# Feed-forward up: the weights' high part against both stream parts in one 512-column matmul

## The chip, the cores and the metric

The kernel runs on one core of one Trainium2 chip. The metric is the device time of one execution in microseconds (us). The engines are named as in the profile: PE (TensorE, matmuls), PEld (its weight loads), DVE (VectorE), ACT (ScalarE), POOL (GpSimd) and SP (SyncE, which here issues most DMAs).

## The reference

A stream x of 256 tokens by 1024 features passes two blocks of two layers each. Every layer of the first block has a mixer and one feed-forward; every layer of the second has a feed-forward, a mixer (state space, then windowed attention), an attention to a memory of 256 tokens and another feed-forward. That makes six feed-forwards. Everything is float32. The lines that matter here:

```python
# first block, per layer: a convolution of width 3 over the tokens on all 2 * 2816 columns
up = depthwise_conv(h @ ffn_w_up[l], ffn_conv_w[l], ffn_conv_b[l])
f = (jax.nn.silu(up[..., :D_FF]) * up[..., D_FF:]) @ ffn_w_down[l]
h = layer_norm(DEEPNORM_ALPHA * h + f, ln_ffn_g[l], ln_ffn_b[l])

# second block, twice per layer
def swiglu(h, wi, wo):
    gate, up = jnp.split(h @ wi, 2, axis=-1)
    return (jax.nn.silu(gate) * up) @ wo
```

D_FF is 2816, so the up projection has 1024 x 5632 weights and the down projection 2816 x 1024.

## The kernel before

All activations stay on the chip, and the weights are streamed once. To keep float32 accuracy, each operand of a matmul is split into a high and a low part (`load` for weights, `split` for activations): ACT rounds the raw values to the high part (L111, a cast), DVE subtracts it from the raw ones for the low part (L112). A product is then three matmuls (`mm3`, L126 to L128): high by high, high by low, low by high.

Weights come in pieces of 1 MB, 128 partitions by 2048 columns. SP issues one DMA for a piece into one of three raw buffers, and ACT and DVE split it in steps of 512 columns (`CUT`) into one of four high and one of four low buffers. A buffer is free again when PE's last matmul on the piece is done.

The stream stands transposed as xh and xl, two tiles of 128 partitions x 8 x 256 (feature tile k, tokens). Each norm writes them through PE transposes into a "tr" bank, which ACT and DVE read out.

The accumulator memory has eight banks of 512 float32 columns: four under the name "acc", two "up", two "tr".

A feed-forward (`ffn`) has 22 blocks b of 128 gate and 128 up columns. Blocks 0 and 1 are made token by token in `first`, since the first token tile is normed earlier than the second. For b from 2 to 21, `up(b)` loads one piece (8 tiles of k by 256 columns), takes one "up" bank of 2 x 256 columns and computes the gate half and the up half of the block in it by `mma`: eight steps of k for each half, and in each step three matmuls with a 128x128 tile of weights as the stationary operand and 256 tokens as the moving one. `evac` reads the bank: with the convolution by one ACT and two DVE operations for each half (L283 to L285); then SiLU on ACT, the product on DVE (L290), and the split into gh and gl, tiles of two blocks that `G[j]` holds.

`down(j, t)` multiplies `G[j]` as the stationary operand with 256 rows of the down projection, 512 columns at a time, for token tile t. The loop over j from 1 to 10 issues two ups and, from j = 2, the down of j - 2; the last two downs follow token tile by token tile, and `fin(t)` adds the residual and norms the tile while PE goes on with the other one. A round below is two ups and one down.

The program is written in the order above. A planner turns it into one queue per engine: it takes the instructions by that order as their operands and buffers come free, by its own costs of each, and sets the semaphores. Each engine then works its queue in order.

Of the kernel before, what the change touches and what calls it, by code (L numbers as in the profile page):

```python
# [26 lines left out]
# order in which the parts of the first block's mixer are issued  # L27
MIX1 = "D0 A0 D1 A1 Q0 v16 Q1 U d1 S0 v18 b1 S1 d0 c b0 o3 a v28 o2"
MIX1_OUT = (1, 0)
# and those of the state-space mixer  # L30
SSD = "t z0 C z1 p0 z2 x0 B x2 x1 p1 e0 x3 w0 w1 y0 z3 o4 o5 e1 p2 p3 o0 o1 w3 y1 w2 o7 o6"
SSD_OUT = (2, 3)
# of the windowed attention and of the attention to the memory
# [3 lines left out]
# column offsets of the packed per-layer input projection of the first block  # L37
WIN_A, WIN_D, WIN_Q, WIN_SV, WIN_U = 0, 4096, 6912, 11008, 13056
# packed rows, read as broadcasts: first block, per layer
BR1 = dict(g6=(0, 384), gcq=(384, 576), gckv=(576, 704), svg=(704, 960), svb=(960, 1216))  # L40
BR1_N = 1216
# second block
BR_SSD = dict(dtb=(0, 16), alog=(16, 32), dsk=(32, 48))
BR_SWA = dict(gq=(0, 64), gk=(64, 128), sink=(128, 144))
# constants that depend on shapes alone
# [3 lines left out]
# per-partition parameters  # L49
# [12 lines left out]
class Kern:  # L62
# [38 lines left out]
    def load(self, src, n):  # L101
        """One piece of a weight stream: raw float32, then the two exact 12-bit parts."""
        nc = self.nc
        k = src.shape[0]
        r = self.wraw.tile([P, 2048], F32, name="wr", tag="wr")[:k, :n]
        nc.sync.dma_start(out=r, in_=src)
        h = self.whi.tile([P, 2048], F32R, name="wh", tag="wh")[:k, :n]
        l = self.wlo.tile([P, 2048], F32R, name="wl", tag="wl")[:k, :n]
        for c in range(0, n, CUT):
            s = slice(c, min(n, c + CUT))  # L110
            nc.scalar.copy(h[:, s], r[:, s])  # L111
            nc.vector.tensor_tensor(out=l[:, s], in0=r[:, s], in1=h[:, s].bitcast(F32), op=ALU.subtract)  # L112
        return h, l

    def loadk(self, src, k, n):
        h, l = self.load(src, k * n)
        return h.rearrange("p (k n) -> p k n", k=k), l.rearrange("p (k n) -> p k n", k=k)
# [5 lines left out]
    def mm3(self, out, sh, sl, mh, ml, first, last):  # L123
        """out += (sh+sl).T @ (mh+ml), the parts being exact."""
        mm = self.nc.tensor.matmul
        mm(out, sh, mh, start=first, stop=False)  # L126
        mm(out, sh, ml, start=False, stop=False)  # L127
        mm(out, sl, mh, start=False, stop=last)  # L128

    def mmb(self, out, t, wp, c0, c1):  # L130
        """Token-major projection of tile t of the stream: out [128 tok, c1-c0]."""
        xh, xl = self.xT
        kk = 0
        for h, l in wp:
            for k in range(h.shape[1]):
                s = slice(t * P, (t + 1) * P)
                self.mm3(out, xh[:, kk, s], xl[:, kk, s], h[:, k, c0:c1], l[:, k, c0:c1], kk == 0, kk == 7)
                kk += 1

    def mma(self, out, wp, c0):  # L140
        """Feature-major projection of 128 columns: out [128 feat, 256 tok]."""
        xh, xl = self.xT
        kk = 0
        for h, l in wp:
            for k in range(h.shape[1]):
                self.mm3(out, h[:, k, c0:c0 + P], l[:, k, c0:c0 + P], xh[:, kk, :], xl[:, kk, :], kk == 0, kk == 7)
                kk += 1

    def rstd(self, ss, n, scale, eps):
        """(ss*scale + eps) ** -0.5 over [128, n], in place."""  # L150
        nc = self.nc
        v = self.wk.tile([P, 8], F32, name="rv", tag="rv", bufs=4)[:, :n]
        r = self.wk.tile([P, 8], F32, name="rr", tag="rr", bufs=4)[:, :n]
        nc.vector.tensor_scalar(out=v, in0=ss, scalar1=scale, scalar2=eps, op0=ALU.mult, op1=ALU.add)  # L154
        nc.gpsimd.tensor_tensor(out=r, in0=v, in1=self.mh[:, 0:1].to_broadcast([P, n]), op=ALU.pow)  # L155
        return r
# [6 lines left out]
    def ln_stats(self, src, width):  # L163
        """mean and rstd of [128, width]"""
        nc = self.nc
        nb = (width + 511) // 512
        st = self.wk.tile([P, 2, 6], F32, name="bst", tag="bst", bufs=3)
        mv = self.wk.tile([P, 2], F32, name="mv", tag="mv", bufs=3)
        for i in range(nb):
            nc.vector.bn_stats(out=st[:, i, :], in_=src[:, i * 512:min(width, (i + 1) * 512)])  # L170
        nc.vector.bn_aggr(out=mv, in_=st[:, :nb, :])
        r = self.rstd(mv[:, 1:2], 1, 1.0, LN_EPS)
        return mv[:, 0:1], r[:, 0:1]

    def new_xT(self):
        self.xT = (self.wk.tile([P, 8, T], F32R, name="xh", tag="xh", bufs=1),
                   self.wk.tile([P, 8, T], F32R, name="xl", tag="xl", bufs=1))

    def transposes(self, src, n, dst_h, dst_l, w=P, rows=P):
        """src [128, n*w] -> dst [w, n, 128] split"""  # L180
        pt = self.bank("tr", [P, 4, P])
        for k in range(n):
            self.nc.tensor.transpose(pt[:w, k, :], src[:, k * w:(k + 1) * w], self.ident)  # L183
        self.split(pt[:w, :n, :], dst_h, dst_l)
# [5 lines left out]
    def norm_ln(self, t, g, b, xT=True):  # L190
        """x[t] <- layer norm of x[t]; then its transposed split"""
        nc, x = self.nc, self.x[t]
        m, r = self.ln_stats(x, D)
        for n in range(2):
            s = slice(n * 512, (n + 1) * 512)
            nc.vector.scalar_tensor_tensor(out=x[:, s], in0=x[:, s], scalar=m, in1=g[:, s], op0=ALU.subtract, op1=ALU.mult)
            nc.vector.scalar_tensor_tensor(out=x[:, s], in0=x[:, s], scalar=r, in1=b[:, s], op0=ALU.mult, op1=ALU.add)
            if xT:
                self.to_xT(x[:, s], n, t)
# [15 lines left out]
    def projector(self, wsrc, nk):  # L215
        """x += oT.T @ w in nk pieces of 256 rows; returns piece(j, oh, ol, kb, tiles) and the banks"""
# [18 lines left out]
    def project(self, oh, ol, wsrc, order, early, fin):  # L235
        """the whole of it; token tile 0 finishes first"""
# [19 lines left out]
    def finisher(self, mode, post, last=False):  # L256
        """post(t): the norm that opens the next stage"""
        def fin(t, acc):
            self.residual(t, acc, mode)
            if t == 0 and not last:  # L260
                self.new_xT()
            post(t)
        return fin

# [1 line left out]
    def ffn(self, wi, wo, conv, fin, nj=11):  # L266
        nc, tc = self.nc, self.tc
        with tc.tile_pool(name="ffn", bufs=2) as fp:
            G = {}

# [39 lines left out]
            def up(b):  # L310
                w = self.loadk(wi[:, b * 2048:(b + 1) * 2048], 8, 256)
                pu = self.bank("up", [P, 2, T])
                for h in range(2):
                    self.mma(pu[:, h], [w], h * P)
                evac(b, pu)
# [5 lines left out]
            def downw(j):  # L321
                WD[j] = self.loadk(wo[:, j * 2048:(j + 1) * 2048], 2, 1024)
# [25 lines left out]
    def softmax(self, sp, sc, nh, w, scale, ri):  # L348
        """sc [128 q, nh, w] in PSUM -> exp(scale*(sc - max)) in SBUF; ri <- 1/sum"""
# [10 lines left out]
    def rope(self, sp, src, nh, q, C, S, out):  # L360
        """out = rotate(src [128, nh, 4q]) with C, S [128, 4q]"""
# [14 lines left out]
    def mixer1(self, l, fin):  # L376
# [3 lines left out]
        with tc.tile_pool(name="mx", bufs=1) as sp:  # L380
# [11 lines left out]
            # A: gated, width-31 convolution over tokens  # L392
# [47 lines left out]
            # D: latent projections  # L440
# [52 lines left out]
            # B: grouped-query attention; heads lie in the order 0 2 1 3  # L493
# [25 lines left out]
            def attend(scores, vget, scale, kb, qt):  # L519
                """scores(u, m, qs): operands of member m of head pair u"""  # L520
# [31 lines left out]
            # C: spatial gating  # L552
# [88 lines left out]
    def xattn(self, i_, fin):  # L641
        nc, tc, a = self.nc, self.tc, self.a
        with tc.tile_pool(name="xa", bufs=1) as sp:
# [9 lines left out]
            def query(i):  # L653
                """query columns of half i // 2, token tile i % 2"""
# [45 lines left out]
            def out(i):  # L700
                """piece i // 2 of the output projection, token tile i % 2"""
# [12 lines left out]
    def ssd(self, fin):  # L714
# [6 lines left out]
        with tc.tile_pool(name="sd", bufs=1) as sp:  # L721
# [19 lines left out]
            def gate_z(i):  # L741
                """silu(z), column half i // 2, token tile i % 2"""
# [15 lines left out]
            def steps(_):  # L758
                """dt = softplus(raw + bias); cumulative sums of dt * a within each chunk"""
# [9 lines left out]
                # log(1 + e) = 2 atanh(e / (2 + e)), |argument| <= 1/3  # L769
# [70 lines left out]
            def decays(g):  # L840
                """exp(acs[l] - acs[s]) * (C B^T), transposed; and the decays to the chunk's end"""
# [23 lines left out]
            def core(g):  # L865
# [6 lines left out]
                # state carried out of the first chunk  # L872
# [29 lines left out]
            # pooling branch  # L902
# [61 lines left out]
    def swa(self, fin):  # L964
        nc, tc, a = self.nc, self.tc, self.a
        tr = nc.tensor.transpose
        with tc.tile_pool(name="sw", bufs=1) as sp:
# [16 lines left out]
            def qkv(i):  # L984
                """column group i // 2 (k and v, then the query halves), token tile i % 2"""
# [32 lines left out]
            def attend(i):  # L1018
                """query tile i // 4, half b of the heads, pair of slot pairs ip"""
# [43 lines left out]
            def out(i):  # L1063
                """piece i // 2 of the output projection, token tile i % 2"""
# [55 lines left out]
def _kmajor(w, c0, c1):  # L1120
    """columns c0:c1 of w [K, N] as [128, K/128, c1-c0]"""
# [8 lines left out]
def _group(w, c0, c1):  # L1130
    """a column group of w [1024, N] as two pieces of four row tiles"""
# [61 lines left out]
def pack(inp):  # L1193
# [4 lines left out]
    pcol = lambda v: v.reshape(-1, P).T  # [.., n*128] -> [128, ..n]  # L1198
# [36 lines left out]
    # heads of the windowed attention, in the order that pairs an even key head with an odd one  # L1235
# [24 lines left out]
```

## Time and profile before

| | us |
|---|---|
| median of 3 runs | 1865.55 |
| the runs | 1864.16, 1865.55, 1871.57 |
| span of the profiled execution | 1871.3 |
| PE busy in it | 1807.8 |
| DVE busy | 1244.9 |
| ACT busy | 1000.6 |

The span runs from the first to the last instruction of the profiled execution. Its own time as a run is not listed apart; the slowest run lies 0.27 us above the span. Busy time is the union of an engine's instructions, and the end of a matmul is modelled, so matmuls that follow each other closely overlap in the rows: their starts tell the pace, not their durations. The mean granted clock of TensorE over the span was 0.989 of full speed.

### The profile page before, as it was taken

The page shows a single profiled execution, that of the slowest core. Times are in us where ns is not written, and L with a number is a line of the kernel's source. Part 1 is how long each engine was busy: PE and PEld are TensorE (multiplying, and loading weights), DVE is VectorE, ACT ScalarE, POOL GpSimd, SP SyncE. Part 2 cuts the span into 40 slices and gives each one's busy share as a digit, 9 for nine tenths or more (in the row PEclk, how much of TensorE's full clock was granted, in tenths as well). Part 3 has the DMA queues.
Part 4 walks back from the last instruction along what each step waited for, and adds up shares of the span by engine and source line. Part 5 has one row for each costly group of instructions (what it writes and reads, how often), then busy time and mean ns, then how long its engine had stood idle before and what let it go on. Part 6 is the DMA issues. An engine that isn't in the chain of part 4 may idle for free.

```text
span 1871.3 us, 29875 instructions
## 1 busy us (share of the span) xinstructions
PE 1807.8 (97%) x11664; PEld 1615.5 (86%) x11664; DVE 1244.9 (67%) x2523; ACT 1000.6 (53%) x2178; POOL 67.1 (4%) x85
## 2 busy tenths in 40 slices
PE   6999999999999999999999999999999999999999
PEld 5777999977899989998988779999999977789998
DVE  6489877778977785555677766545645566775553
ACT  5565655556565554445674555444544457655442
POOL 0000000010000000000000000000000010000000
PEclk9999999999999999999999999999999999999999
DMA  8623755442765545554434536555555552435551
GB/s 312 209 94 110 248 181 180 150 163 68 236 203 180 191 161 191 181 187 162 141 119 147 182 136 214 183 187 194 169 183 194 186 189 102 158 135 188 197 182 68
DMA packets 50750, 320.93 MB, mean 172 GB/s; under 512 B 5616, under 2 KB 8560, under 8 KB 14896
## 3 DMA queue, kind: packets, MB, share of 16 engines
q1 hardware_dynamic: 46160, 311.63, 48.6%
q10 hardware_dynamic: 4448, 7.37, 1.2%
q8 instruction: 92, 1.51, 0.3%
q14 instruction: 50, 0.41, 0.1%
HBM read 315.84 MB, written 3.15 MB: 170 GB/s over the span
## 4 chain that ended last, share of the span: by engine, by line
PE 82%; DVE 9%; ACT 4%; POOL 2%; issue 2%; DMA 1%; SPq 0%; POOLq 0%; ACTq 0%
PE up L128 14%; PE up L126 14%; PE up L127 14%; PE acc L127 11%; PE acc L128 11%; PE acc L126 11%; DVE wl L112 3%; POOL rr L155 2%; PE tr L183 2%; ACT wh L111 1%; DVE ca L418 1%; DMA wr<-in_ffn_w_up_dram 1%; DVE xn L212 1%; PE up L1053 1%; PE up L539 1%
## 5 line engine op out<-in xcount | busy, mean ns | idle before, releaser
L112 DVE TENSOR_TENSOR wl<-wr,wh 128x512 fp32r<-128x512 f32 x1135 | 737.1, 682 | 416.6 <-ACT wh L111 412.2
L111 ACT CAST wh<-wr 128x512 fp32r<-128x512 f32 x1135 | 644.9, 618 | 499.3 <-issue 298.5
L128 PE MATMUL up<-xh,wl 128*128 128x256 f32 x2112 | 601.5, 285 | 3.9 <-DVE wl L112 3.9
L126 PE MATMUL up<-xh,wh 128*128 128x256 f32 x2112 | 602.4, 285 | 0.0
L127 PE MATMUL up<-xl,wh 128*128 128x256 f32 x2112 | 600.3, 284 | 0.0
L128 PEld LDWEIGHTS up<-xh,wl 128*128 128x128 f32 x2112 | 408.0, 193 | 5.1 <-DVE wl L112 4.9
L126 PEld LDWEIGHTS up<-xh,wh 128*128 128x128 f32 x2112 | 408.3, 193 | 2.5 <-issue 0.2
L127 PEld LDWEIGHTS up<-xl,wh 128*128 128x128 f32 x2112 | 408.0, 193 | 2.4
L128 PE MATMUL acc<-wh,gl 128*128 128x512 f32 x528 | 208.7, 395 | 0.0
L127 PE MATMUL acc<-wl,gh 128*128 128x512 f32 x528 | 208.4, 395 | 0.0
L126 PE MATMUL acc<-wh,gh 128*128 128x512 f32 x528 | 208.2, 394 | 0.0
L127 PE MATMUL acc<-wl,xh 128*128 128x512 f32 (+2 forms) x336 | 130.0, 388 | 0.4 <-DVE wl L112 0.4
L126 PE MATMUL acc<-wh,xh 128*128 128x512 f32 (+2 forms) x336 | 129.5, 389 | 0.4 <-ACT xh L120 0.3
L128 PE MATMUL acc<-wh,xl 128*128 128x512 f32 (+2 forms) x336 | 128.6, 384 | 0.0
L128 PEld LDWEIGHTS acc<-wh,gl 128*128 128x128 f32 x528 | 99.4, 188 | 23.0
L126 PEld LDWEIGHTS acc<-wh,gh 128*128 128x128 f32 x528 | 99.7, 189 | 20.7
L127 PEld LDWEIGHTS acc<-wl,gh 128*128 128x128 f32 x528 | 99.4, 188 | 20.7
L155 POOL TENSOR_TENSOR rr<-rv,mh 128x1 f32<-128x1 f32 (+4 forms) x66 | 59.2, 898 | 1483.1 <-DVE rv L154 1460.1
L120 ACT CAST gh<-g 128x256 fp32r<-128x256 f32 x132 | 53.4, 406 | 58.3 <-DVE g L290 58.3
L126 PEld LDWEIGHTS acc<-wh,xh 128*128 128x128 f32 x336 | 64.5, 192 | 11.6 <-ACT xh L120 1.3
L127 PEld LDWEIGHTS acc<-wl,xh 128*128 128x128 f32 x336 | 64.4, 192 | 10.7 <-DVE wl L112 0.9
L128 PEld LDWEIGHTS acc<-wh,xl 128*128 128x128 f32 x336 | 64.4, 192 | 10.2
(323 smaller groups left out, 2217.7 us busy)
## 6 DMA issues: line engine op xcount, KB each, us to landing
wr<-in_ffn_wi_dram SPq DMA_DIRECT2D x88, 1024.0 KB, 4.9
wr<-in_ffn_w_up_dram SPq DMA_DIRECT2D x44, 1024.0 KB, 5.0
wr<-in_ffn_wo_dram SPq DMA_DIRECT2D x44, 1024.0 KB, 4.8
wr<-in_ffn_w_down_dram SPq DMA_DIRECT2D x22, 1024.0 KB, 4.8
wr<-in_ssd_in_dram SPq DMA_DIRECT2D x14, 1024.0 KB, 4.9
wr<-in_w_in_dram SPq DMA_DIRECT2D x12, 1024.0 KB, 4.8
wr<-in_mem_wkv_dram SPq DMA_DIRECT2D x8, 1024.0 KB, 6.9
wr<-in_w_out_dram SPq DMA_DIRECT2D x8, 1024.0 KB, 4.9
```

The source lines that it names most:

```text
L111: nc.scalar.copy(h[:, s], r[:, s])
L112: nc.vector.tensor_tensor(out=l[:, s], in0=r[:, s], in1=h[:, s].bitcast(F32), op=ALU.subtract)
L120: self.nc.scalar.copy(hi, src)
L126: mm(out, sh, mh, start=first, stop=False)
L127: mm(out, sh, ml, start=False, stop=False)
L128: mm(out, sl, mh, start=False, stop=last)
L155: nc.gpsimd.tensor_tensor(out=r, in0=v, in1=self.mh[:, 0:1].to_broadcast([P, n]), op=ALU.pow)
L183: self.nc.tensor.transpose(pt[:w, k, :], src[:, k * w:(k + 1) * w], self.ident)
L212: nc.vector.scalar_tensor_tensor(out=xn, in0=x[:, s], scalar=r[:, 0:1], in1=g[:, s], op0=ALU.mult, op1=ALU.mult)
L418: nc.vector.scalar_tensor_tensor(out=ca[:, b], in0=aT[:, b, k:k + T], scalar=w, in1=ca[:, b], op0=ALU.mult, op1=ALU.add)
L539: nc.tensor.matmul(po[:, (2 * u + m) * 64:(2 * u + m + 1) * 64], pT[:, m * 2 + kt, :], vget(u, m, kt), start=kt == 0, stop=kt == 1)
L1053: nc.tensor.matmul(po[:, sl[m], :], pT[:, m, kt, :], v[kt][:, kv * 64:(kv + 1) * 64], start=kt == 0, stop=kt == qt)
```

## The change

The stream's two parts become one tile `xhl` of 128 partitions x 8 x 2 x 256, so that for each k the 256 tokens of the high part and the 256 of the low part lie side by side; xh and xl are views of it. In `up`, `mma` is replaced by `mmw`: for each k one matmul of the high weights with all 512 columns, into a whole bank, and one of the low weights with the high part, into the bank's second half. The two halves of a block now have a bank each, one from "up" and one from "tr". At the read-out (`halves`) ACT copies the bank's second half and DVE adds the first half to it, into a tile that `evac` then reads in place of the bank. The pieces of up blocks 2 to 21 and of the down projection are split in steps of 1024 columns in place of 512. Comments are dropped throughout.

```diff
-    def load(self, src, n):
+    def load(self, src, n, cut=CUT):
...
-        for c in range(0, n, CUT):
-            s = slice(c, min(n, c + CUT))
+        for c in range(0, n, cut):
+            s = slice(c, min(n, c + cut))
             nc.scalar.copy(h[:, s], r[:, s])
             nc.vector.tensor_tensor(out=l[:, s], in0=r[:, s], in1=h[:, s].bitcast(F32), op=ALU.subtract)
...
+    def mmw(self, out, w, c0):
+        mm, (h, l) = self.nc.tensor.matmul, w
+        for k in range(8):
+            mm(out, h[:, k, c0:c0 + P], self.xhl[:, k], start=k == 0, stop=False)
+            mm(out[:, 1], l[:, k, c0:c0 + P], self.xT[0][:, k, :], start=False, stop=k == 7)
...
     def new_xT(self):
-        self.xT = (self.wk.tile([P, 8, T], F32R, name="xh", tag="xh", bufs=1),
-                   self.wk.tile([P, 8, T], F32R, name="xl", tag="xl", bufs=1))
+        self.xhl = self.wk.tile([P, 8, 2, T], F32R, name="xhl", tag="xhl", bufs=1)
+        self.xT = self.xhl[:, :, 0, :], self.xhl[:, :, 1, :]
...
+            def halves(p):
+                t = fp.tile([P, 2, T], F32, name="hs", tag="hs", bufs=2)
+                u = fp.tile([P, 2, T], F32, name="up_s", tag="up_s", bufs=2)
+                for h in range(2):
+                    nc.scalar.copy(t[:, h], p[h][:, 1])
+                    nc.vector.tensor_tensor(out=u[:, h], in0=p[h][:, 0], in1=t[:, h], op=ALU.add)
+                return u
...
             def up(b):
-                w = self.loadk(wi[:, b * 2048:(b + 1) * 2048], 8, 256)
-                pu = self.bank("up", [P, 2, T])
+                w = self.loadk(wi[:, b * 2048:(b + 1) * 2048], 8, 256, 1024)
+                pu = [self.bank(tag, [P, 2, T]) for tag in ("up", "tr")]
                 for h in range(2):
-                    self.mma(pu[:, h], [w], h * P)
-                evac(b, pu)
+                    self.mmw(pu[h], w, h * P)
+                evac(b, halves(pu))
...
             def downw(j):
-                WD[j] = self.loadk(wo[:, j * 2048:(j + 1) * 2048], 2, 1024)
+                WD[j] = self.loadk(wo[:, j * 2048:(j + 1) * 2048], 2, 1024, 1024)
```

## Rows read from the trace of the kernel before

**Rows 1.** The page's part 1: busy us, share of the span, instructions.

```profile
PE 1807.8 (97%) x11664; PEld 1615.5 (86%) x11664; DVE 1244.9 (67%) x2523; ACT 1000.6 (53%) x2178; POOL 67.1 (4%) x85
```

**Rows 2.** The page's part 4: engines' shares of the chain that ended last.

```profile
PE 82%; DVE 9%; ACT 4%; POOL 2%; issue 2%; DMA 1%; SPq 0%; POOLq 0%; ACTq 0%
```

**Rows 3.** Busy time by stage, two stretches inside feed-forwards.

```profile
core 0: us, PE busy (x) PEld busy (x) DVE busy (x) ACT busy (x) POOL busy (x), PEclk, DMA share, GB/s
...
200.00:350.00 150.00, 150.00 (x1073) 141.56 (x1073) 115.29 (x226) 89.57 (x185) 0.00 (x0) 1.00 0.57 190
...
700.00:850.00 150.00, 150.00 (x1074) 141.51 (x1073) 79.44 (x146) 68.57 (x144) 0.00 (x0) 1.00 0.54 182
```

**Rows 4.** ACT's waits from 200 to 350: us in total, times, longest.

```profile
ACT wh L111 <- PE up L127: 28.9, 11, 3.4
ACT gh L120 <- DVE g L290: 25.5, 14, 2.1
```

**Rows 5.** The page's part 5, up matmuls: busy us, mean ns, idle before.

```profile
L126 PE MATMUL up<-xh,wh 128*128 128x256 f32 x2112 | 602.4, 285 | 0.0
L126 PEld LDWEIGHTS up<-xh,wh 128*128 128x128 f32 x2112 | 408.3, 193 | 2.5 <-issue 0.2
```

**Rows 6.** PE's timeline from 305.5: start us, duration us, what.

```profile
305.67 0.28 PE L128 MATMUL up<-xh,wl 128*128 128x256 f32 x1
305.79 0.39 PE L126 MATMUL acc<-wh,gh 128*128 128x512 f32 x1
306.02 0.39 PE L127 MATMUL acc<-wl,gh 128*128 128x512 f32 x1
...
310.20 0.40 PE L127 MATMUL acc<-wl,gh 128*128 128x512 f32 x1
310.44 0.40 PE L128 MATMUL acc<-wh,gl 128*128 128x512 f32 x1
...
311.13 0.40 PE L128 MATMUL acc<-wh,gl 128*128 128x512 f32 x1
311.37 0.28 PE L126 MATMUL up<-xh,wh 128*128 128x256 f32 x1
311.49 0.28 PE L127 MATMUL up<-xl,wh 128*128 128x256 f32 x1
...
322.76 0.28 PE L128 MATMUL up<-xh,wl 128*128 128x256 f32 x1
322.88 0.39 PE L126 MATMUL acc<-wh,gh 128*128 128x512 f32 x1
```

**Rows 7.** Groups by line and shape, whole span: busy us, mean ns.

```profile
L302 ACT COPY u<-up 128x256 f32<-128x256 f32 x24 | 8.9, 372 | 22.7 <-PE up L128 22.6
...
L290 DVE TENSOR_TENSOR g<-sg,up 128x256 f32<-128x256 f32 x80 | 33.1, 414 | 2.5 <-ACT sg L288 2.5
...
L1069 DVE TENSOR_TENSOR x<-x,gb 128x1024 f32<-128x1024 f32 x2 | 2.4, 1197 | 0.0
```

**Rows 8.** Groups by line and shape from 200 to 350.

```profile
L112 DVE TENSOR_TENSOR wl<-wr,wh 128x512 fp32r<-128x512 f32 x108 | 70.6, 684 | 23.7 <-ACT wh L111 22.0
L111 ACT CAST wh<-wr 128x512 fp32r<-128x512 f32 x107 | 60.2, 617 | 30.6 <-PE up L127 28.9 <-PE acc L128 1.7
...
L120 ACT CAST gh<-g 128x256 fp32r<-128x256 f32 x20 | 8.1, 404 | 25.5 <-DVE g L290 25.5
```

**Rows 9.** Timeline at a feed-forward's entry, DVE and PE.

```profile
1315.91 1.88 DVE L112 TENSOR_TENSOR wl<-wr,wh 128x512 fp32r<-128x512 f32 x3
...
1320.48 0.63 PE L183 MATMUL tr<-ck,xn 128*128 128x128 f32 x4 [0.43 <-DVE xn L212]
```

More of the change, by code (lines that the diff above doesn't have):

```diff
@@ L113, in load, with loadk @@
         return h, l
-    def loadk(self, src, k, n):
-        h, l = self.load(src, k * n)
+    def loadk(self, src, k, n, cut=CUT):
+        h, l = self.load(src, k * n, cut)
         return h.rearrange("p (k n) -> p k n", k=k), l.rearrange("p (k n) -> p k n", k=k)
```

## The prediction

> **What bounds the kernel now.** I read the busy shares first: TensorE's matmuls fill 97% of the span, VectorE two thirds, ScalarE about half [rows 1]. The chain of work that ended last says the same from the other side: 82% of it is PE, 9% DVE [rows 2]. The table by stage is the view that decides. In two stretches of 150 us inside feed-forwards, one with the convolution (200 to 350) and one without (700 to 850), PE is busy all 150 us at the full granted clock (1.00), while DVE has 115.3 and 79.4 us and ACT 89.6 and 68.6 us of work [rows 3]. So a feed-forward goes at PE's pace, and what PE sheds there is shed from the end, as long as nothing else becomes late.
>
> The waits of ACT in the convolved stretch say who is ahead: ACT's cast L111 waited 28.9 us, 11 times, for PE's matmul L127 [rows 4]. That is a cast with no free weight buffer: it may only go on when PE has finished a piece four pieces back. The splitting of weights runs as far ahead as its buffers let it, and idle time of this kind is slack.
>
> **How matmuls are to be counted.** The group rows give an up matmul a mean of 285 ns [rows 5], and it is tempting to say that two matmuls of 256 columns (570 ns) become one of 512 (0.39 us on the timeline), 175 ns less a step. That would be more than twenty times too much, for the durations overlap: the timeline shows starts 0.12 us apart in the up stage, and 0.23 to 0.24 us apart in the down stage [rows 6]. From the first down matmul at 305.79 to the first up at 311.37 are 24 matmuls of 512 columns: 5.58 us, 232.5 ns each. From there to the next down matmul at 322.88 are 96 of 256 columns: 11.51 us, 119.9 ns each. Twice the columns cost 112.6 ns more, so about 112.6 ns go with 256 columns and 7.3 ns are fixed per matmul, whatever its width. The weight loads do not show beside this: 0.19 us each, they lie inside these steps.
>
> **The change part by part.** One step of k in an up is now three matmuls of 256 columns; after, one of 512 (high weights against both stream parts) and one of 256 (low weights against the high part). The columns streamed are the same 768. Only one matmul's fixed cost goes: 3 x 119.9 = 359.7 ns becomes 232.5 + 119.9 = 352.4 ns, 7.3 ns less. There are 20 ups per feed-forward (b = 2 to 21; b = 0 and 1 go another way and stay), 2 halves, 8 steps, 6 feed-forwards: 1920 steps, the greater part of the 2112 instructions of that row [rows 5]. 1920 x 7.3 ns = 14.0 us. The stretch holds PE alone, so all of it is on the path: one round (two ups and one down) falls from 17.09 to 16.86 us. The bounds of the pair come from the same rows: at the 0.24 us that some 512-column starts are apart it is 0.36 and gains nothing (0); at 0.22, a hundredth under the 0.23 that the rows also show, it would be 0.34 and gain 38 us. I take the mean, because 24 equal steps make it and the pair is of the same two kinds. Removed with it are 1920 weight loads, which cost nothing now and give nothing back.
>
> A rule of the Trainium skill (page "TensorE: Matmul & The Clock Gate", section "Back-to-back issue gap") speaks against the change: a matmul at the full clock takes N/2.4 ns plus about 2.5 ns, so that merging two saves only 2.5 ns. By it the gain would be an estimated 1920 x 2.5 = 4.8 us and the time 1860.8 us. The rows differ from it in both places, 119.9 ns against its 109.2 and 232.5 against its 215.8, so I hold to the rows.
>
> The read-out. For each half of an up, ACT copies 256 columns out of the bank and DVE adds the bank's other 256. The nearest rows are ACT's copy of 256 columns from an up bank, 372 ns, and DVE's product of one SBUF and one bank operand, 414 ns [rows 7]. With four halves in a round that is +1.49 us of ACT and +1.66 us of DVE.
>
> The split of weights in pieces of 1024 in place of 512. A DVE operation on 1024 columns is in the trace, 1197 ns [rows 7], against 684 for 512 [rows 8]: the twelve subtractions of a round become six, 8.21 us become 7.18, -1.03 us. ACT's casts are 617 ns for 512 and 404 for 256 [rows 8], so 0.83 ns a column; 1024 is an estimated 1043 ns, and 7.40 us become 6.26, -1.15 us.
>
> Together a round has DVE +0.63 and ACT +0.34 us. Now it has, by 17.09/150 of the stretches [rows 3], 13.1 and 10.2 us with the convolution, 9.1 and 7.8 without; after, 13.8 and 10.5, or 9.7 and 8.1, in 16.86. PE covers all of it, so I cost it at nothing. If the cover were gone, it would cost between 0 and 0.63 x 60 rounds = 38 us. The chain from the last matmul of an up to its G gets longer by copies and adds, but G is first read by the down two rounds on, and at the end behind another down (5.58 us): nothing. In return the first half's bank can be read while PE still fills the second half's, since they are now different banks.
>
> The banks. An up holds one "up" and one "tr" bank, two of each, so still two ups are in flight; the transposes of the norms, which share "tr", come only before the first and after the last up. PE would wait if a bank's two reads (about 0.8 us) were not over one up (5.6 us) later. Nothing. No DMA is added, moved or dropped, and SP's queue keeps its order. The stream's two parts in one tile: the same writes and reads, at other addresses: nothing.
>
> The edges. A piece's first part is ready later, 1.04 + 1.20 in place of 0.62 + 0.68 us, +0.94 us. At a feed-forward's entry the pieces 0 and 1 keep the cut of 512, and those that stand in DVE's queue between the second tile's norm steps (three, 1.88 us) are theirs, which cost PE 0.43 us of idle time there [rows 9]. I cost this at 0, with ends from -0.94 to +0.94 us for each of twelve edges, 11 us either way.
>
> **The sum** against the profiled execution: span 1871.3 - 14.0 = 1857.3. That profile is at the slow end of the runs (1864.16 to 1871.57; the slowest is 0.27 above its span, which I take as what lies around it). Taken from the median, 1865.55 - 14.0 = **1851.5 us**.
>
> **The rivals.**
> *The edges take part of it back.* The engines' order is planned from a list and its costs; other instructions can change it around the norms and in the mixers, where PE does wait (63.5 us of the span [rows 1]). For: DVE's x norms at the edges stand behind weight subtractions, and those get longer. Against: the ones that stand there keep their size. Six to twelve edges at 0.94 us: 1857 to 1863, say 1860.
> *The pair is not cheaper*, so the change doesn't do what it says: the 512-column matmul of the up takes 0.24 us, or the fixed part is less than 7.3 ns. For: some starts of such a matmul are 0.24 us apart [rows 6], and 7 ns in 230 is a thin margin. Against: 24 of them average 232.5. At 0.24 us for each nothing is gained, 1865.5; halfway there, 1858.5. On this side lies the rule of the Trainium skill cited above (page "TensorE: Matmul & The Clock Gate", section "Back-to-back issue gap"), with its estimate of 1860.8.
> *Slower: VectorE becomes the bound in the two convolved feed-forwards.* Its queue is in order. If its present idle time, 34.7 of 150 us or 3.95 us a round, were all forced and each of the four adds also waited out its copy (4 x 0.372 = 1.49 us), a round would last 13.74 + 3.95 + 1.49 = 19.18 us against 17.09: +2.09 x 20 rounds = +42, less 40 x 0.234 = 9.4 gained in the other four: +32, 1898 us. It begins to bite past 16.86 us a round and makes the whole slower past 17.09 + 9.4/20 = 17.56. For: DVE would be at 82% there. Against: 22.0 of the 34.7 us is the subtraction waiting for its cast [rows 8], and the casts wait for buffers that PE frees [rows 4]; that slack is used up first.
>
> **How the numbers follow.** The forecast has 0.57 (its own range 1845 to 1857), the edges 0.20, the pair 0.10, VectorE 0.13. A measurement of this kernel tells about 0.5%, 9.3 us, from no change: faster is under 1856.2, slower over 1874.9. Faster: 0.57 and 0.03 of the edges, 0.60. Same: 0.17 + 0.10 + 0.02 of VectorE's mild cases, 0.29. Slower: 0.11. The range goes from 1842 (12 ns a step in place of 7.3) to 1872, where it takes in the edges, the dear pair and the mildest of VectorE.
>
> **What would show it.** In the up stage, starts after a 512-column matmul 0.23 us and after a 256-column one 0.12 us apart, and a round of 16.86 us; PE busy without a gap inside the feed-forwards, DVE near 82% in the convolved ones; 1024-column subtractions near 1.2 us. I am wrong if PE waits there for weight parts or for banks, if the pair takes 0.36 us, or if the mixers' stretches change their length though their code did not.

## The result, and the profile after

The changed kernel takes 1842.9 to 1853.8 us in five runs (one more run, at 0.56 of the clock, is left out of the comparison); before stood at a median of 1867.5 us beside them. The ratio is 0.9898, 95% interval 0.9874 to 0.9922: 14.6 to 23.5 us less, 19.0 by its centre. Run again on another occasion it gave 0.9916 (0.9903 to 0.9930), 15.7 us less. The forecast was 14.0 us less and 1851.5 us; the five runs have a median of 1852.7.

The page's first part, answering to [rows 1]:

```profile
PE 1775.0 (96%) x9744; PEld 1496.8 (81%) x9744; DVE 1305.0 (71%) x2391; ACT 1061.6 (58%) x2046; POOL 67.5 (4%) x85
```

1920 matmuls and as many weight loads are gone; DVE and ACT have some 60 us more to do each, and the kernel is faster all the same. The table by stage, same stretches and columns as [rows 3]:

```profile
200.00:350.00 150.00, 150.00 (x797) 128.21 (x796) 125.43 (x212) 99.35 (x173) 0.00 (x0) 1.00 0.56 193
700.00:850.00 150.00, 150.00 (x789) 127.69 (x788) 88.36 (x128) 77.69 (x126) 0.00 (x0) 1.00 0.54 186
```

PE still fills both. DVE's share with the convolution went from 77% to 84%, without from 53% to 59%. The first matmul of four downs in PE's timeline (start, duration), and the steps of two ups ahead of the second and the third, answering to [rows 6]:

```profile
217.39 0.39 PE L126 MATMUL acc<-wh,gh 128*128 128x512 f32 x1
...
231.30 0.39 PE L155 MATMUL tr<-xhl,wh 128*128 128x512 f32 x1
231.53 0.27 PE L156 MATMUL tr<-xhl,wl 128*128 128x256 f32 x1
231.64 0.40 PE L155 MATMUL tr<-xhl,wh 128*128 128x512 f32 x1
...
232.33 0.40 PE L155 MATMUL tr<-xhl,wh 128*128 128x512 f32 x1
...
234.07 0.39 PE L126 MATMUL acc<-wh,gh 128*128 128x512 f32 x1
...
245.28 0.40 PE L155 MATMUL up<-xhl,wh 128*128 128x512 f32 x1
245.51 0.28 PE L156 MATMUL up<-xhl,wl 128*128 128x256 f32 x1
245.63 0.40 PE L155 MATMUL up<-xhl,wh 128*128 128x512 f32 x1
...
246.34 0.40 PE L155 MATMUL up<-xhl,wh 128*128 128x512 f32 x1
...
250.93 0.39 PE L126 MATMUL acc<-wh,gh 128*128 128x512 f32 x1
...
267.61 0.39 PE L126 MATMUL acc<-wh,gh 128*128 128x512 f32 x1
```

The rounds last 16.68, 16.86, 16.68 us and go on in turn, in all six feed-forwards. In a short round three steps take 1.03 us (231.30 to 232.33), in a long one 1.06 (245.28 to 246.34). Over whole ups it is 346.5 ns a step in the one and 353.3 in the other, where the three matmuls of before took 359.7. Mean 16.77 against 17.09 us: 0.32 x 60 rounds = 19.2 us.

The groups by line and shape that answer to [rows 7] and [rows 8], over the whole span:

```profile
L112 DVE TENSOR_TENSOR wl<-wr,wh 128x1024 fp32r<-128x1024 f32 x372 | 449.3, 1221 | 260.6 <-ACT wh L111 259.7
L111 ACT CAST wh<-wr 128x1024 fp32r<-128x1024 f32 x372 | 383.9, 1049 | 138.6 <-PE tr L155 78.1 <-PE acc L128 49.7 <-DMA wr<-in_ffn_w_up_dram 8.1
L286 DVE TENSOR_TENSOR up_s<-tr,hs 128x256 f32<-128x256 f32 x120 | 50.2, 419 | 7.5 <-ACT hs L285 7.5
L286 DVE TENSOR_TENSOR up_s<-up,hs 128x256 f32<-128x256 f32 x120 | 50.2, 418 | 0.2 <-ACT hs L285 0.2
L285 ACT COPY hs<-up 128x256 f32<-128x256 f32 x120 | 44.5, 370 | 68.9 <-PE up L156 68.9
```

The prices taken from neighbouring rows held: 1221 for 1197 ns, 1049 for 1043, 419 for 414, 370 for 372.

The two profiled spans, 1871.3 and 1841.1 us, are 30 us apart, more than the times. The mean granted clock was 0.989 in the one and 0.997 in the other. What that is worth can be read from runs of one kernel: the kernel before, in its runs beside experiment 1, took 1874.5 us at a clock of 0.989 (mean of three) and 1863.2 at 0.996 (mean of five), so 1.6 us go with each 0.001, and an estimated 13 us with the 0.008 between the two spans. The clock is lost between the feed-forwards, not in the stretches above: from 100 to 200 us, in a mixer, it was 0.97 before and 1.00 after. The repeat of the changed kernel, profiled at 0.990, has a span of 1852.5: 18.8 us under before at nearly the same clock, which is the 19.2 us of the rounds less a little at the edges.

### The profile page after: what moved, and what is told of

It reads as the page before. It is cut to its first block, busy times and chain, and to the rows that moved or that the text cites. A ratio compares the mean times of both kernels' runs of the same rounds, so it can differ in the third digit from the quotient of the medians.

```text
span 1841.1 us, 25714 instructions
## 1 busy us (share of the span) xinstructions
PE 1775.0 (96%) x9744; PEld 1496.8 (81%) x9744; DVE 1305.0 (71%) x2391; ACT 1061.6 (58%) x2046; POOL 67.5 (4%) x85
## 4 chain that ended last, share of the span: by engine, by line
PE 81%; DVE 9%; ACT 4%; POOL 2%; issue 2%; DMA 1%; SPq 0%; POOLq 0%; ACTq 0%
PE tr L155 12%; PE up L155 12%; PE acc L127 11%; PE acc L128 11%; PE acc L126 11%; PE tr L156 6%; PE up L156 6%; DVE wl L112 3%; POOL rr L164 2%; PE up L128 2%; PE up L126 2%; PE up L127 2%; PE tr L192 2%; ACT wh L111 1%; DVE xn L221 1%
## 5 line engine op out<-in xcount | busy, mean ns | idle before, releaser
L112 DVE TENSOR_TENSOR wl<-wr,wh 128x512 fp32r<-128x512 f32 (+1 forms) x763 | 702.0, 944 | 307.0 <-ACT wh L111 305.5
L111 ACT CAST wh<-wr 128x512 fp32r<-128x512 f32 (+1 forms) x763 | 602.9, 828 | 206.7 <-PE acc L128 91.1
L155 PE MATMUL up<-xhl,wh 128*128 128x512 f32 x960 | 342.0, 396 | 0.0
L155 PE MATMUL tr<-xhl,wh 128*128 128x512 f32 x960 | 340.9, 396 | 0.0
L156 PE MATMUL up<-xhl,wl 128*128 128x256 f32 x960 | 267.6, 279 | 0.0
L156 PE MATMUL tr<-xhl,wl 128*128 128x256 f32 x960 | 267.6, 279 | 0.0
L155 PEld LDWEIGHTS up<-xhl,wh 128*128 128x128 f32 x960 | 180.2, 188 | 42.2
L156 PEld LDWEIGHTS up<-xhl,wl 128*128 128x128 f32 x960 | 180.7, 188 | 2.1
L156 PEld LDWEIGHTS tr<-xhl,wl 128*128 128x128 f32 x960 | 180.8, 188 | 0.0
L126 PE MATMUL acc<-wh,xhl 128*128 128x512 f32 (+2 forms) x336 | 128.1, 385 | 0.4 <-ACT xhl L120 0.3
L128 PE MATMUL acc<-wh,xhl 128*128 128x512 f32 (+2 forms) x336 | 127.2, 380 | 0.0
```

Source lines behind the costliest of these rows:

```text
L155: mm(out, h[:, k, c0:c0 + P], self.xhl[:, k], start=k == 0, stop=False)
L156: mm(out[:, 1], l[:, k, c0:c0 + P], self.xT[0][:, k, :], start=False, stop=k == 7)
```

## The experiments

**1. Three matmuls again, all else changed.** Tells the matmul from the read-out, the split and the order.

```diff
-            mm(out, h[:, k, c0:c0 + P], self.xhl[:, k], start=k == 0, stop=False)
+            mm(out[:, 0], h[:, k, c0:c0 + P], self.xT[0][:, k, :], start=k == 0, stop=False)
+            mm(out[:, 1], h[:, k, c0:c0 + P], self.xT[1][:, k, :], start=False, stop=False)
```

> The changed kernel, with its banks, read-out, stream tile and split of 1024, but the 512-column matmul is two of 256 again (three matmuls a step, the same 768 columns, the bank's two halves filled as in the change). Theory M (the gain is the fixed cost of one matmul in each of 1920 steps): starts 0.12 us apart again, a round of 17.09 us in place of a mean of 16.77, and the time back at that of before, 1866 to 1869 us, ratio 0.999 to 1.002. Rival S (the gain, or the part of it above the predicted 14 us, comes from the read-out, the wider split or the planner's order): the time stays 5 us or more under before, ratio 0.997 or less, though the round is 17.09.

Measured: ratio 1.0013 (0.9997 to 1.0029). PE's timeline, two downs one round apart:

```profile
236.15 0.28 PE L157 MATMUL tr<-xhl,wl 128*128 128x256 f32 x1
236.27 0.28 PE L155 MATMUL tr<-xhl,wh 128*128 128x256 f32 x1
236.39 0.28 PE L156 MATMUL tr<-xhl,wh 128*128 128x256 f32 x1
236.51 0.28 PE L157 MATMUL tr<-xhl,wl 128*128 128x256 f32 x1
236.63 0.39 PE L126 MATMUL acc<-wh,gh 128*128 128x512 f32 x1
...
253.71 0.39 PE L126 MATMUL acc<-wh,gh 128*128 128x512 f32 x1
```

0.12 us a matmul, 17.08 us a round. The gain is the merged matmul together with the weight load that goes with it; what was changed around it gives nothing that this comparison, good to some 3 us, can tell.

**2. The wider split alone**, in the kernel before (`load` and `loadk` get the last argument as in the change).

```diff
...
-                w = self.loadk(wi[:, b * 2048:(b + 1) * 2048], 8, 256)
+                w = self.loadk(wi[:, b * 2048:(b + 1) * 2048], 8, 256, 1024)
...
-                WD[j] = self.loadk(wo[:, j * 2048:(j + 1) * 2048], 2, 1024)
+                WD[j] = self.loadk(wo[:, j * 2048:(j + 1) * 2048], 2, 1024, 1024)
```

> The kernel before with the split of up and down pieces in steps of 1024 alone. Theory M: PE's round stays 17.09 us and the time is that of before within 3 us, ratio 0.998 to 1.002; DVE has 1.0 us a round less to do, which nobody waits for. Rival S: 5 us or more faster (ratio 0.997 or less), from norm steps that stand behind less work, or 2 to 3 us slower, if the wider pieces stand in the way at the entries.

Measured: 1.0018 (1.0002 to 1.0034), no gain and perhaps 3 us of loss. Set beside runs of before at the same clock, 0.989, 0.991 and 0.992, its means differ by -0.3, 2.5 and 0.6 us, so the loss is not shown. Rounds are 17.09 us as expected.

**3. No read-out.**

```diff
...
-                    gate, upv = pu[:, 0], pu[:, 1]
+                    gate, upv = (pu[0][:, 0], pu[1][:, 0]) if isinstance(pu, list) else (pu[:, 0], pu[:, 1])
...
+                        ph = pu[h][:, 0] if isinstance(pu, list) else pu[:, h]
...
-                evac(b, halves(pu))
+                evac(b, pu)
```

In the convolution the three operations read `ph` in place of `pu[:, h]`.

> The changed kernel without the read-out: no copy and no add, the rest reads the first half of each bank alone, so the products with the second half are computed and left out of the result. Theory M: PE's round as in the change (mean 16.77 us) and the time of the changed kernel within 3 us, ratio to before 0.988 to 0.992: the 1.5 us of ACT and 1.7 us of DVE a round lie beside PE. Rival S or the VectorE rival: faster than the changed kernel by 5 us or more (ratio 0.987 or less), most of it in the two convolved feed-forwards.

Measured: 0.9909 (0.9885 to 0.9932), rounds of 16.68 and 16.86 us: the changed kernel's time without its copies and adds. They cost nothing that the rounds show, nor the time within some 4 us.

**4. The eight wide matmuls of a half first, then the eight narrow ones.**

```diff
         for k in range(8):
             mm(out, h[:, k, c0:c0 + P], self.xhl[:, k], start=k == 0, stop=False)
+        for k in range(8):
             mm(out[:, 1], l[:, k, c0:c0 + P], self.xT[0][:, k, :], start=False, stop=k == 7)
```

> The changed kernel with the order of the matmuls of one half changed: first the eight of 512 columns, then the eight of 256, the same sixteen. By the additive sum of the prediction (232.5 and 119.9 ns whatever stands next to it) a step is 352.4 ns and the round 16.86 us, in every round: 1920 x 7.3 = 14 us under before, ratio 0.9925, 4 to 5 us over the changed kernel. By the rival (a step's time is what the two kinds cost next to each other: 346.5 ns in every second round of the changed kernel's trace, 353.3 in the others) the excess comes from the alternation, and all rounds of this kernel are alike at 16.86. If the rounds alternate here too, at 16.68 and 16.86, the order has nothing to do with it.

Measured: 0.9906 (0.9885 to 0.9926). Both theories missed: all rounds are alike, as the rival said, but at 16.75 us, not 16.86. PE's timeline with like rows merged:

```profile
232.13 2.00 PE L155 MATMUL up<-xhl,wh 128*128 128x512 f32 x8
233.97 1.12 PE L157 MATMUL up<-xhl,wl 128*128 128x256 f32 x8
234.92 2.00 PE L155 MATMUL tr<-xhl,wh 128*128 128x512 f32 x8
```

Eight of 512 columns from 232.13 to 233.97 are 230 ns each, eight of 256 to 234.92 are 119. The wide matmul is 2.5 ns cheaper here than in the down stage, where its moving operand is a weight and its stationary one an activation.

**5. Split of 512 in the changed kernel** (`loadk` without the last argument in both places).

> The changed kernel with the split of all weights back in steps of 512. The split of 1024 alone made the kernel before 0.18% slower, so by theory E (the wide pieces stand in the way of norm steps at the entries and ends of feed-forwards, 2 to 3 us in all, and nothing else of the split matters) this one is about 3 us under the changed kernel: ratio to before 0.986 to 0.990, mean round 16.77 us as in the change, DVE 0.8 to 1.0 us a round busier. By the VectorE rival the extra work of DVE in the convolved rounds (near 15 of 16.77 us) makes PE wait: rounds over 16.9 us there, and no gain.

Measured: 0.9896 (0.9878 to 0.9914), rounds as in the change. All six runs had a clock of 0.989 and a mean of 1852.6 us. The changed kernel has three runs at this clock, from other occasions: 1853.4, 1853.5 and 1856.5, 1.9 us more in the mean. So few runs neither show theory E, which expected 2 to 3 us, nor rule it out; a cost of the wide split of some 2 us stays open. The VectorE rival is ruled out: no round is over 16.9 us.

**6. Grouped order and split of 512 together.**

> Both edits together: the eight 512-column matmuls of a half first, then the eight of 256, and the split in steps of 512. Rounds of 16.75 us, all alike, as with the grouping alone; by theory E 2 to 3 us under the changed kernel, ratio to before 0.987 to 0.990. If it is at 0.991 or over, the split is not what cost.

Measured: 0.9876 (0.9854 to 0.9897), rounds of 16.75 us.

**7 and 8. More work for VectorE**: the slower rival, tested by its own point.

```diff
-                evac(b, halves(pu))
+                u = halves(pu)
+                for i in range(1):
+                    for h in range(2):
+                        v = fp.tile([P, T], F32, name="vx", tag="vx", bufs=2)
+                        nc.vector.tensor_tensor(out=v, in0=u[:, h], in1=u[:, h], op=ALU.add)
+                evac(b, u)
```

The second kernel has `range(2)`, that of experiment 9 `range(4)`.

> The changed kernel with two more adds of 256 columns on DVE in each up (four a round), whose results nobody reads: DVE's work of a convolved round goes from 14.0 to about 15.7 us of PE's 16.77. By the prediction's reading (idle time of DVE there is slack) rounds stay at a mean of 16.77 and the time is the changed kernel's, ratio to before 0.989 to 0.993. By the VectorE rival (its idle time, now 2.75 us a round, is forced) a convolved round becomes about 18.4 us, 20 of them 33 us more: ratio 1.005 to 1.010.

> The same with four more adds in each up (eight a round): DVE's work of a convolved round is about 17.4 us, over PE's 16.77, so DVE must become the bound there: rounds of 17.4 us if its slack can all be used, 12 us more in the 20 convolved rounds, ratio to before 0.996 to 0.999; up to 20.1 us a round and 67 us more, ratio 1.026, if its idle time stays. The four feed-forwards without the convolution (9.9 + 3.3 us) keep a mean round of 16.77.

Measured: 0.9897 (0.9876 to 0.9918) and 0.9882 (0.9853 to 0.9911). Neither costs anything that the times show. The second kernel's convolved stretch, columns as before:

```profile
200.00:350.00 150.00, 149.29 (x792) 127.14 (x791) 146.03 (x286) 99.14 (x171) 0.00 (x0) 1.00 0.56 193
```

and PE's waits in it (us in total, times, longest):

```profile
PE acc L127 <- DVE wl L112: 0.7, 1, 0.7
```

DVE is busy 146 of 150 us and PE has waited once. My 17.4 us a round was too high by the price of an add. An add lasts 418 ns in the rows, but operations that follow each other overlap there: 73 adds raised DVE's busy time in the stretch from 125.4 to 146.0 us, 0.28 us each, so eight make 2.3 us a round and DVE has 16.3 of 16.77. Nearly all of it went into idle time: from the first down matmul to the last the two convolved feed-forwards take 152.6 and 151.5 us, 0.8 more than in the changed kernel.

**9. Eight more adds in each up.**

> The changed kernel with eight more adds on DVE in each up (sixteen a round), results unread. With four in each up DVE was busy 146.0 of 150 us in the convolved stretch, 16.3 us a round, and PE waited 0.7 us there. Eight more adds a round of 0.33 to 0.42 us make 19.0 to 19.7 us, over PE's 16.77: DVE must now set the pace of the convolved rounds, 20 x 2.2 to 2.9 = 45 to 58 us more than the changed kernel, ratio to before 1.013 to 1.022. Without the convolution it is 13.0 + 3 = 16 us, still under PE: those rounds stay at 16.77. If the convolved rounds stay at 16.77 too, DVE's rows do not tell its limit.

Measured: 1.0124 (1.0094 to 1.0154). The stretches and PE's waits in the first of them:

```profile
200.00:350.00 150.00, 137.36 (x713) 115.35 (x713) 147.79 (x322) 87.22 (x151) 0.00 (x0) 0.99 0.44 156
700.00:850.00 150.00, 143.10 (x779) 123.00 (x779) 135.96 (x263) 77.16 (x131) 3.79 (x4) 0.98 0.56 197
```

```profile
PE up L156 <- DVE wl L112: 10.3, 6, 4.2
PE acc L126 <- ACT wh L111: 2.3, 1, 2.3
```

Here the rival is real: DVE sets the pace with the convolution, and PE waits for weight parts, the low ones above all, a sign that the prediction's last paragraph names. From the first down matmul to the last a convolved feed-forward takes 171.7 and 171.2 us, where the changed kernel takes 151.8 and 150.6: 20 us more in each, 40 of the 42 us between the two ratios. Where its rounds can be told apart they last 17.8 to 19.0 us. The planner gave PE another order there too (four wide matmuls of both halves ahead of a narrow one, from 300.93 on), so the cost is that of the adds with the order that came of them. It takes an extra sixteen adds a round to get there. Without the convolution the rounds stay at 16.68 and 16.86 us (the second stretch here is shifted and holds an edge, hence POOL's 3.8 us).

**10. Two wide, two narrow, with the split of 512.**

```diff
-        for k in range(8):
-            mm(out, h[:, k, c0:c0 + P], self.xhl[:, k], start=k == 0, stop=False)
-            mm(out[:, 1], l[:, k, c0:c0 + P], self.xT[0][:, k, :], start=False, stop=k == 7)
+        for k in range(0, 8, 2):
+            for i in range(2):
+                mm(out, h[:, k + i, c0:c0 + P], self.xhl[:, k + i], start=k + i == 0, stop=False)
+            for i in range(2):
+                mm(out[:, 1], l[:, k + i, c0:c0 + P], self.xT[0][:, k + i, :], start=False, stop=k + i == 7)
...
```

> The kernel with the split of 512 throughout and the matmuls of an up in fours: two of 512 columns (k, k+1), then two of 256. Additive theory from the down's row: 232.5 and 119.9 whatever the order, a round of 16.86. If a 512-column matmul of the up costs about 230 by itself, as in the grouped order, 349 ns a step and 16.75 in all rounds. If the neighbours decide, rounds between 16.68 and 16.86 that depend on where the round starts, as in the changed kernel, whose steps are 346.5 or 353.3 ns.

Measured once: 1849.5 us. Rounds are 16.71 to 16.74 us, about 348 ns a step:

```profile
248.46 0.62 PE L156 MATMUL up<-xhl,wh 128*128 128x512 f32 x2
248.93 0.40 PE L158 MATMUL up<-xhl,wl 128*128 128x256 f32 x2
249.16 0.63 PE L156 MATMUL up<-xhl,wh 128*128 128x512 f32 x2
```

Two wide ones 0.47 us, two narrow ones 0.23. Over the whole run, waits left out, that is 233 and 115 ns each, where eight in a row are 230 and 119: neighbours do matter, by a few ns, and here in opposite directions.

**11 and 12. The changed kernel and the grouped one side by side.**

> The changed kernel itself, to stand on the same chip beside the grouped one. Rounds of 16.68 and 16.86 us in turn, ratio to before 0.989 to 0.991 by 60 rounds x 0.31 us = 19 us less 1 to 2 us at the edges.

> The grouped order with the split of 512 once more, beside the changed kernel on the same chip. If the split of 1024 costs 2 to 3 us (the kernel before was 0.18% slower with it), this is 2 to 4 us under the changed kernel; if that was a chance of the chip, the two are within 1.5 us of each other, since their mean rounds are 16.75 and 16.77.

Measured: 0.9916 (0.9903 to 0.9930) and 0.9877 (0.9858 to 0.9896). The grouped order with the split of 512 beats both kernels on that occasion, 1845.8 against 1854.7 us, but its rounds explain 60 x 0.02 = 1 us of the 9. Its runs had granted clocks of 0.989 to 0.996, the changed kernel's 0.988 to 0.990; at 1.6 us for 0.001, the 0.004 between the means are an estimated 6 us. Some 2 us are left, too little to assign. Whether the order keeps the clock up or chance did is open: in experiment 4 the same order with the wide split ran at 0.990 to 0.991.

## Why the prediction was right, and where its size was off

**PE is the bound in a feed-forward**: right. PE has no gap in the stretches of after, and the time follows the rounds. One sign of being wrong did show, mixers that change their length, but the clock did that: from the third feed-forward's last down to the fourth's first are 283.8 us before (0.96 of the clock between 876 and 1137), 277.5 after (0.99) and 283.8 in the repeat (0.96).

**Count by starts, not by durations**: right, and it decided the forecast. By durations the saving would have been 175 ns a step and over 300 us.

**The pair's price**: the term that was mis-sized. I took 7.3 ns a step, "because 24 equal steps make it and the pair is of the same two kinds". Measured are 13.2 and 6.4 ns in turn (359.7 less 346.5 and 353.3), 9.8 on average, so 19 us and not 14.0. The sum took 232.5 ns for the wide matmul and 119.9 for the narrow one; in the changed kernel their starts are 233 and 116 apart in the mean, waits left out, so it is the narrow one behind a wide one that came out cheaper. Grouped by kind they are 230 and 119 (experiment 4), in sum 349 to the pair's 350: order moves the price between the two and hardly changes the sum. The 24 equal steps fixed the price of one stage only. Rows of before that the forecast did not use have the same shape at another price, in the projection of the memory's values at the kernel's start, at the full granted clock:

```profile
52.04 0.39 PE L126 MATMUL acc<-wh,xh 128*128 128x512 f32 x1
...
57.48 0.39 PE L126 MATMUL acc<-wh,xh 128*128 128x512 f32 x1
```

These are 24 matmuls in 5.44 us, 226.7 ns each; with that price the saving would have been 13.1 ns a step and 25 us. So the trace of before gave 14 to 25 us, and the measured 19 lies between.

**One matmul's fixed cost**: that a matmul less saves time is shown; that the cost is the matmul's and not that of its weight load is not. Every matmul here brings a load (9744 of each), and no run takes away the one alone. The prediction had the loads lie inside the steps, but a load lasts 0.19 us in the rows and a step of 256 columns 0.12. Nor does a fixed part of 7 to 10 ns hold for narrower matmuls: in the changed kernel's state-space mixer 32 of 64 columns take 3.50 us, 109 ns each, at the full granted clock.

```profile
955.05 3.68 PE L907 MATMUL up<-xr,E 128*128 128x64 f32 x32
958.55 0.48 PE L126 MATMUL acc<-wh,ph 128*128 128x512 f32 x1
```

**The rule of the Trainium skill** (page "TensorE: Matmul & The Clock Gate", section "Back-to-back issue gap"), 2.5 ns a matmul: the runs decide against it here, with 9.8 ns saved for each matmul merged. The section gives this figure for a matmul by itself, which the prediction left out.

**The read-out costs nothing**: right (experiment 3). So is the bank count: PE has no wait at all in either stretch.

**The edges at 0, ends 11 us either way**: right in size, and the small rest is a loss. At clocks of 0.990 and 0.989 the repeat's runs lie 17.5 and 18.2 us under those of before beside them, where the rounds alone give 19.2. One entry got worse, that of the first feed-forward of the second block, where two norms follow each other. PE's timeline with its wait in brackets, before and after:

```profile
689.45 1.29 PE L183 MATMUL tr<-ck,xn 128*128 128x128 f32 x8 [0.40 <-DVE xn L212]
679.01 1.19 PE L192 MATMUL tr<-ck,xn 128*128 128x128 f32 x7 [1.83 <-DVE xn L221]
```

In the repeat this wait is 0.65 us. All PE waits for a norm's xn are 22.8 us before, 25.5 after and 23.8 in the repeat.

**VectorE as the bound**: did not occur, and experiments 7 to 9 put the point where it does between eight extra adds a round, which cost next to nothing, and sixteen. Its "all idle time is forced" was wrong; the argument against it (casts wait for buffers that PE frees) was the right one.

**The sum against the profile**: I took 0.27 us for what lies around the span. Runs with a span of their own show 1.8 (1842.93 against 1841.1), so the profile of before stood for a run slower than any listed. The sum from the median was not touched by that. That this sum came within 2 us of the median measured is in part luck: the saving was 5 us larger by the ratio's centre, and the median of before, with three more runs, 1.9 us higher than the one it started from.

## What to carry to other kernels

Price a matmul by the distance of starts in a stretch without gaps, and expect from a merge of two with the same columns only what does not go with the columns, here about 10 ns in 240 for two of 256. Take the price from every stage that has the shape, and the spread between them as the range. A few ns per matmul depend on what stands beside it, so for a change that lives on that term keep the range at half to double. Work moved onto engines that wait for the bound one was free here until their busy time nearly filled the round (146 of 150 us), and the way to know the reserve is to add work until it costs.

## What was not expected of the hardware

The same sequence of sixteen matmuls of 512 and 256 columns in turn runs at one of two paces, 346.5 or 353.3 ns a pair, keeps it for a whole round and changes with the next down (16.68 and 16.86 us, both at the full granted clock). In the trace's nanoseconds the starts repeat every two pairs in the short rounds (about 231, 112, 233, 117) and every three in the long ones (235, 114, 232, 118, 241, 120). Grouping the widths gives one pace, 349 ns a pair, and two of each in turn 348. What sets the pace is open.
